# An adaLN modulation moved from VectorE to TensorE, and the softmax division to ScalarE, in a two-layer trunk on one core

## The chip, the core and the metric

The kernel runs on one core of one Trainium2 chip. The metric is the device time of one execution in microseconds (us). The core has five engines with queues of their own: TensorE (PE: matmuls, with its weight loads shown apart as PEld), VectorE (DVE), ScalarE (ACT), GpSimd (POOL) and SyncE (SP), which here issues nearly all transfers from main memory.

## What is computed

The input is 256 tokens of 1,024 float32 values. Layer 0 has an S5 state-space mixer, layer 1 an attention mixer (FoX: softmax attention with a forget gate, 16 heads of 64). Each mixer is followed by a mixture-of-experts block (MoE) of 32 experts in 4 groups, of which a token uses 2. Before each of the four there is a norm and a modulation (adaLN) whose shift and scale come from one conditioning vector c; a gate from c multiplies the result. Keys, values and the forget gate have a norm and a modulation of their own.

```python
def adaln(c, w, b, n):
    mod = jax.nn.silu(c) @ w + b
    return jnp.split(mod, n, axis=-1)

def modulate(h, shift, scale):
    return h * (1.0 + scale[:, None, :]) + shift[:, None, :]
...
    h = modulate(rmsnorm(x, kv_g), shift, scale)
    k, v, fz = jnp.split(h @ kv_w, [D_MODEL, 2 * D_MODEL], axis=-1)
...
    logf = jax.nn.log_sigmoid(fz.astype(jnp.float32) + kv_fb.astype(jnp.float32))
    fcum = jnp.cumsum(logf, axis=1).transpose(0, 2, 1)
...
        logits = (jnp.einsum('bhqd,bhkd->bhqk', qb, kb).astype(jnp.float32) * scale
                  + fcum[:, :, s0:s1, None] - fcum[:, :, None, :s1])
        mask = (s0 + jnp.arange(Q_BLOCK))[:, None] >= jnp.arange(s1)[None, :]
        p = jax.nn.softmax(jnp.where(mask, logits, NEG), axis=-1)
        outs.append(jnp.einsum('bhqk,bhkd->bhqd', p.astype(vb.dtype), vb))
    o = jnp.concatenate(outs, axis=2).transpose(0, 2, 1, 3).reshape(bsz, seq, D_MODEL)
    return (o * jax.nn.sigmoid(og)) @ w_o
```

## The kernel before

**Weights and the ring.** All weights are read once, in 280 blocks of 128 partitions x 8 KB (1 MB each), through a ring of slots. `fetch` takes the next slot and issues the transfer on SyncE's queue (L67), which works in order: a transfer whose slot is not free yet holds up all behind it. The ring has 12 slots; `grow` adds slots where other memory has come free, `shrink` takes them back. `block` fetches a block when it is wanted and `prefetch` earlier. For the second MoE, `load(1)` prefetches expert weights (`wa`, `wb`) as far as there are slots.

**The order of the work.** In the attention stage TensorE's instructions keep the order of the program (`manual_schedule`); those of the other engines and the transfers are put in order by a planner that goes by a model of their times. The order of TensorE is written out in calls near the end of `trunk`: both halves of K (`project(hk, n, head_norm(kn))`), both of V, both of Q, four output gates (`out_gate`), four parts of the output projection (`out_proj`). Small work is put between the matmuls of these loops by generators in the list `between`; `tick` moves the first of them on by one `yield`. `step(ada)` moves on the modulations that are made on TensorE.

**Quarters.** The projections run as float32r products of a high and a low part. `quarter` hands out 512 columns of a weight block at a time: ScalarE copies the high part (L1125), VectorE subtracts it from the weights for the low part (L1126). The last four blocks, `wo`, are first multiplied by a gate on GpSimd (L1123). Up to three quarters stand ready.

**Modulations.** `ada_cols_pe` makes a shift or a scale on TensorE: 64 matmuls over four blocks (L169), and a few VectorE operations that bring the result into columns (`as_columns`). `ada_gate_pe` makes a gate (L184, then L194 and L195). The last shift and scale, those of the second MoE (`ada11`, sets 0 and 1), are made on VectorE instead: `silu_row` spreads silu(c) over a tile (L203, L205), and `ada_cols_v` takes for each 1,024 columns one sum of products (L214), 16 in all. `quarter` calls one such sum at every 9th, later every 4th and 3rd turn; each holds its block's slot until its second sum.

**Normed input.** `hn_parts` transposes the normed tokens (L1153), modulates them (L1160, L1162) and writes high and low parts (L1164, L1165). For K and V it calls `forget_logits` on each chunk as well: small matmuls of 16 columns against `smallw` (L1189), ahead of K's projection (L1200). `forget_gates` takes the logits from there to the running sums.

**Softmax.** `weights(hg)` does one group of four heads, in two query tiles: logits (L1310), mask and maximum on VectorE (L1313, L1317), exponentials on ScalarE (L1319), reciprocal (L1321) and division (L1322) on VectorE. `turned_weights` transposes the result (L1336) and copies it out of PSUM, two of three copies on ScalarE (L1342) and one on VectorE (L1340). `turned_heads` turns keys and queries (L1285), with one of four copies on VectorE (L1289).

In the MoE of layer 0 the ring has slots on the left side of the memory and five on its right; in that of layer 1 on the left alone. Tiles of 8 KB stand one behind another, so all slots of one side begin at the same offset within 256 bytes.

Of the kernel before, what the change touches and what calls it, by code (L numbers as in the profile page):

```python
# [10 lines left out]
F32 = mybir.dt.float32  # L11
# [3 lines left out]
AF = mybir.ActivationFunctionType  # L15
# [4 lines left out]
D = 1024  # L20
T = 256
KD = 8
NE = 32
CAP = 32
NQ = NE // 4
EPS = 1e-6
BIG = 1e30
# [11 lines left out]
def trunk(ctx: ExitStack, tc: tile.TileContext, A, out, ring=12, ring2=4, ring3=5, ring4=3, ring5=4, lpb=2, TK=2):  # L39
# [3 lines left out]

    const = ctx.enter_context(tc.tile_pool(name="const", bufs=1))
    small = ctx.enter_context(tc.tile_pool(name="small", bufs=2))
    wpool = ctx.enter_context(tc.tile_pool(name="ring", bufs=ring))
    slots = [wpool] * ring
    turn_ = [0]
# [126 lines left out]
    def ada_gate_pe(name, j, li, gbc, at_once=False):  # L175
# [16 lines left out]
        for n in range(2):  # L192
            pt = mm_tile()
            PE.matmul(pt, pick[:, n:n + 1].to_broadcast([128, 128]), rows, start=True, stop=True)  # L194
            S.activation(gbc[:, 512 * n:512 * n + 512], pt, AF.Copy)  # L195

    def silu_row(pool):

        o = pool.tile([128, D], F32, name="scr")
        for n in range(2):  # L200
            pt = mm_tile()
            for k in range(4):
                PE.matmul(pt[:, 128 * k:128 * k + 128], sc[:, 4 * n + k:4 * n + k + 1].to_broadcast([128, 128]), ident,  # L203
                          start=True, stop=True)
            S.activation(o[:, 512 * n:512 * n + 512], pt, AF.Copy)  # L205
        return o

    def ada_cols_v(name, j, sc_row, dst, bias, lng=None):

        for b in range(4):  # L210
            w = block(name, j, b)
            for c in range(2):
                wc = w[:, 1024 * c:1024 * c + 1024]
                V.tensor_tensor_reduce(wc, wc, sc_row, 1.0, 0.0, op0=OP.mult, op1=OP.add,  # L214
                                       accum_out=dst[:, 2 * b + c:2 * b + c + 1])
                yield
        V.tensor_tensor(dst, dst, cols[:, bias:bias + 8], op=OP.add)
        if lng is not None:
            V.scalar_tensor_tensor(dst, dst, 1.0, cols[:, lng:lng + 8], op0=OP.add, op1=OP.mult)

    def as_shift(bias, sh):
        return lambda ps: as_columns(ps, 8, sh, cols[:, bias:bias + 8])
# [855 lines left out]
    def add_square(i, n, src):  # L1078
# [1 line left out]
        square(ssq2, i, n)  # L1080

    gb11 = gate_tile(small)
    A2 = [1, 1, 1, 1]
    M.experts(mosti, fill, add_square)


# [7 lines left out]
    gb10 = gate_tile(tp)  # L1094
    ada = [ada_cols_pe("ada10", 0, as_shift(C_ADAB + 32, sh10)),
           ada_cols_pe("ada10", 1, as_gain(C_ADAB + 32, C_LNG + 16, g10)), ada_gate_pe("ada10", 2, 2, gb10, True)]
    fill = [ada_gate_pe("ada11", 2, 3, gb11)]
    later.extend(("ada11", (j, b)) for j in range(2) for b in range(4))
    turns = [0]
    VP = [9, 9, 4, 3]  # L1100


    todo = [("wk", n, kh) for n in range(2) for kh in range(2)] + [("wv", n, kh) for n in range(2) for kh in range(2)]
# [25 lines left out]
    def quarter():  # L1129

        while len(ready) < 3 and (todo or rest_blocks or rest):
            split_next()
        turns[0] += 1
        if turns[0] % VP[turns[0] // 20 % 4] == 0:
            step(vwork)
        return ready.pop(0)


# [4 lines left out]
            while between and next(between[0], 0) == 0:  # L1143
                between.pop(0)

    def hn_parts(xs, sh, g, also=None):

        o = tp.tile([128, KD, 2, T], F32R, tag="hn", name="hn", bufs=1)
        pts = [mm_tile() for _ in range(4)]
        for i in range(2):  # L1150
            for k in range(KD):
                at = 256 * (k % 2) + 128 * i
                PE.transpose(pts[k // 2][:, at:at + 128], xs[:, i, 128 * k:128 * k + 128], ident)  # L1153
        for kk in range(4):
            xf = tp.tile([128, 2, T], F32, tag="xf", name="xf", bufs=2)
            for k2 in range(2):
                k = 2 * kk + k2
                src = pts[kk][:, 256 * k2:256 * k2 + 256]
                if k2:
                    V.tensor_scalar(xf[:, k2], src, g[:, k:k + 1], sh[:, k:k + 1], op0=OP.mult, op1=OP.add)  # L1160
                else:
                    S.activation(xf[:, k2], src, AF.Identity, bias=sh[:, k:k + 1], scale=g[:, k:k + 1])  # L1162
            hi, lo = o[:, 2 * kk:2 * kk + 2, 0, :], o[:, 2 * kk:2 * kk + 2, 1, :]
            S.activation(hi, xf, AF.Copy)  # L1164
            V.tensor_tensor(lo, xf, hi.bitcast(F32), op=OP.subtract)  # L1165
            if also:
                also(kk, xf)
        return o

    in_order = ExitStack()  # L1170
# [1 line left out]
    xs = tp.tile([128, 2, D], F32, tag="xs", name="xs", bufs=1)  # L1172
    for i in range(2):
        rms(ssq2, xs, i)
    scr = silu_row(tp)
    vwork = [ada_cols_v("ada11", 0, scr, sh11, C_ADAB + 48),
             ada_cols_v("ada11", 1, scr, g11, C_ADAB + 56, C_LNG + 24)]
    kn = ap.tile([128, 2, 16, 66], F32, name="kn")
    qn = ap.tile([128, 2, 16, 66], F32, name="qn")
    v = vp.tile([128, 2, D], F32, name="v")  # L1180
    G.memset(kn[:, :, :, 65:66], 1.0)
    G.memset(qn[:, :, :, 64:65], 1.0)
    pz = acc_tile()

    def forget_logits(kk, x):
        for k2 in range(2):
            k = 2 * kk + k2
            for i in range(2):
                PE.matmul(pz[:, 16 * i:16 * i + 16], x[:, k2, 128 * i:128 * i + 128], smallw[:, k, 0:16],  # L1189
                          start=k + i == 0, stop=k == KD - 1, skip_group_check=True)  # L1190

    hk = hn_parts(xs, shkv, gkv, forget_logits)

    def project(src, n, use):
        pk = [acc_tile() for _ in range(2)]
# [40 lines left out]

    def forget_gates():

        def a32(n):
            return ap.tile(t32, F32, name="f_" + n)  # L1240

        fz, fa, fe, fs, f2, fp = (a32(n) for n in ("z", "a", "e", "s", "2", "p"))
        V.tensor_tensor(fz, pz[:, 0:32], cols[:, C_FBR:C_FBR + 32], op=OP.add)
        V.tensor_scalar(fa, fz, -1.0, None, op0=OP.mult)
        V.tensor_tensor(fa, fa, fz, op=OP.min)
        yield
# [29 lines left out]
    def turned_heads(hg):  # L1276

        ts = hts[hg] = []
        for src, nm in ((kn, "kA"), (qn, "qA")):

            dst = ap.tile([66, 4, T], F32, tag=nm, name=nm, bufs=1)
            for i in range(2):
                pt = mm_tile()
                for j in range(4):
                    PE.transpose(pt[:66, 128 * j:128 * j + 128], src[:, i, 4 * hg + j, :], ident)  # L1285
                o = dst[:, :, 128 * i:128 * i + 128]
                s = pt[:66, :].rearrange("p (a t) -> p a t", a=4)
                if nm == "kA" and i:
                    V.tensor_copy(o, s)  # L1289
                elif nm == "kA":  # L1290
                    S.activation(o, s, AF.Copy)
                else:
                    S.activation(o, s, AF.Copy, scale=gqk[:66])
                yield
            ts.append(dst)
    def weights(hg):
# [3 lines left out]
        for qt in range(2):  # L1300
# [18 lines left out]
                S.activation(pr[:, j], pr[:, j], AF.Exp, bias=mx[:, j:j + 1], accum_out=sm[:, j:j + 1])  # L1319
            yield  # L1320
            V.reciprocal(sm, sm)  # L1321
            V.tensor_tensor(pr, pr, sm[:, :, None].to_broadcast([128, 4, w]), op=OP.mult)  # L1322
        yield

    def turned_weights(hg):

        prs = hps.pop(hg)
        if hg > 1:
            while hg - 2 not in done:
                yield  # L1330
        pT = vp.tile([128, 4, 3, 128], F32, tag="pT", name="pT", bufs=2)
        for qt in range(2):
            for kb in range(qt + 1):
                pp = mm_tile()
                for j in range(4):
                    PE.transpose(pp[:, 128 * j:128 * j + 128], prs[qt][:, j, 128 * kb:128 * kb + 128], ident)  # L1336
                dst = pT[:, :, qt + kb, :]
                src = pp.rearrange("p (a t) -> p a t", a=4)
                if kb:
                    V.tensor_copy(dst, src)  # L1340
                else:
                    S.activation(dst, src, AF.Copy)  # L1342
                if qt + kb < 2:
                    yield
        pTs[hg] = pT
# [86 lines left out]
    project(hk, 1, head_norm(kn))  # L1432
    step(ada)
    project(hk, 0, use_v)
    step(ada)
    project(hk, 1, use_v)
    tick(99)
    hq = hn_parts(xs, sh10, g10)
    sgT = tp.tile([128, 8, T], F32, tag="xs", name="sgT", bufs=1)
    project(hq, 0, head_norm(qn))  # L1440
    between += [turned_heads(0), weights(0)]
    step(ada, A2[0])
    project(hq, 1, head_norm(qn))
    for hg in range(1, 4):
        between += [both(turned_heads(hg), turned_weights(hg - 1)), weights(hg)]
    between += [release(), turned_weights(3)]
    step(ada, A2[1])
    out_gate(0)
    step(ada, A2[2])
    out_gate(1)  # L1450
    step(ada, A2[3])
    values(0)
    out_gate(2)
    values(1)
# [3 lines left out]
    split_values(0)  # L1458
    split_values(1)
    out_proj(0)  # L1460
    step(ada, 99)
    values(2)
    split_values(2)
    out_proj(1)
# [4 lines left out]
    grow(er, "ring5", ring5, first=True)  # L1469
    ahead_of_moe()  # L1470
    out_proj(2)
    step(vwork, 99)
    c36 = router(1, sh11, g11)
    out_proj(3)
    in_order.close()
# [25 lines left out]
def layouts(x, c, ln_g, ada_w, ada_b, s5_w_in, s5_lambda_re, s5_lambda_im, s5_log_dt, s5_b_re, s5_b_im,  # L1501
# [69 lines left out]
        return w.reshape(8, 128, n, 256).transpose(2, 1, 0, 3).reshape(n, 128, 2048)  # L1571

    d = {"x": np.asarray(x)[0], "cols": cols, "smallw": smallw, "s5b": s5b, "s5c": s5c}
    def over(w):

        return w.T.reshape(4, 2, 128, D).transpose(0, 2, 1, 3).reshape(4, 128, 2 * D)

    def sets(w, turned=()):
        return np.stack([over(w[:, D * j:D * j + D]) if j in turned else rows(w[:, D * j:D * j + D], 2)
                         for j in range(w.shape[1] // D)])  # L1580

    d["gbias"] = ab[:, 2 * D:].reshape(4, 2, 512)
    d["ada00s"], d["ada00g"] = rows(aw[0][:, :2 * D], 1), sets(aw[0][:, 2 * D:])
    d["ada01"], d["ada10"], d["ada11"] = sets(aw[1]), sets(aw[2]), sets(aw[3], (0, 1))
    d["kvada"] = sets(np.asarray(kv_ada_w))
    d["win"] = bands(np.asarray(s5_w_in[0]))
    w = np.asarray(s5_w_out[0])
# [26 lines left out]
```

## Time and profile before

| | |
|---|---|
| Median of 3 runs | 838.55 us (837.41 to 838.63) |
| The profiled execution: its time | 838.87 us |
| Its span, first to last instruction | 837.1 us |
| Busy TensorE, VectorE, ScalarE, GpSimd | 710.3, 412.0, 218.8, 51.8 us |
| Granted TensorE clock, mean | 0.932 |
| Read from main memory | 297.31 MB |

The span is what the profile's rows cover; 1.8 us of the profiled execution's time lie around it. Busy times of different engines overlap. Instructions of one engine overlap a little too, so that the mean duration of one times their number can exceed the busy time; four matmuls on different column groups run side by side.

### The profile page before, as it was taken

The numbers are of one execution on the slowest core, as the hardware profiler recorded it, in microseconds if no ns is written. First come the engines' busy times: TensorE is split into PE (matmuls) and PEld (weight loads), VectorE is DVE, ScalarE is ACT, GpSimd is POOL, SyncE is SP. The second block draws the span as 40 slices with busy tenths as digits, with TensorE's granted clock in tenths as the row PEclk, the third lists the DMA queues.
The fourth block names the chain that finished last, engine by engine and source line by source line (L and its number), as shares of the span: only waits on it lengthen the run. The fifth ranks groups of instructions, "written<-read, shape, count | busy, mean of one in ns | idle before, by whom it ended". The sixth has DMA issues, their size and how long they took to land. (4 is left out here: it accounts for less than half of the span.)

```text
span 837.1 us, 13449 instructions
## 1 busy us (share of the span) xinstructions
PE 710.3 (85%) x5396; PEld 407.1 (49%) x5396; DVE 412.0 (49%) x1068; ACT 218.8 (26%) x498; POOL 51.8 (6%) x52
## 2 busy tenths in 40 slices
PE   3897999897899987676799988599998999887776
PEld 0674776584343333131286776488764333331311
DVE  7685999864422221120376589967654222221202
ACT  4332333252211110010234355456522111100100
POOL 2000000000000000000002106900000000000000
PEclk9998999998999999898769999789999999997887
DMA  9998956778999999999999996323879999999996
GB/s 370 418 417 346 385 175 254 302 300 324 418 419 420 419 418 420 420 417 416 421 418 377 412 380 230 128 104 105 350 313 404 418 420 419 419 420 419 417 413 251
DMA packets 41827, 299.28 MB, mean 358 GB/s; under 512 B 4632, under 2 KB 4760, under 8 KB 5664
## 3 DMA queue, kind: packets, MB, share of 16 engines
q1 hardware_dynamic: 41344, 297.14, 87.5%
q10 hardware_dynamic: 416, 1.23, 0.4%
q8 instruction: 44, 0.72, 0.3%
q14 instruction: 23, 0.19, 0.1%
HBM read 297.31 MB, written 1.05 MB: 356 GB/s over the span
## 5 line engine op out<-in xcount | busy, mean ns | idle before, releaser
L506 PE MATMUL mm<-w,xg 128*32 128x512 f32 x1024 | 144.3, 645 | 28.7 <-DMA w<-wa 10.9
L506 PEld LDWEIGHTS mm<-w,xg 128*32 128x32 f32 x1024 | 29.8, 112 | 118.2 <-issue 68.1
L478 ACT ACTIVATE xg<-mm,sh,g 128x128 f32<-128x128 f32 x64 | 29.3, 458 | 189.0 <-PE mm L470 172.8
L521 PE MATMUL mm<-w,aT 128*32 128x512 f32 x512 | 68.0, 647 | 12.5 <-DMA w<-wb 6.9
L1200 PE MATMUL acc<-ws,hn 128*128 128x512 f32 x288 | 74.2, 416 | 2.3 <-ACT hn L1164 2.3
L1126 DVE TENSOR_TENSOR ws<-w,ws 128x512 fp32r<-128x512 f32 x80 | 60.9, 765 | 29.6 <-ACT ws L1125 29.3
L470 PE MATMUL mm<-Pr,h 128*128 128x128 f32 x512 | 64.2, 279 | 11.2 <-DVE Pr L458 11.2
L470 PEld LDWEIGHTS mm<-Pr,h 128*128 128x128 f32 x512 | 59.8, 192 | 26.0 <-issue 18.6
L528 PE MATMUL acc<-y,Sc 128*128 128x512 f32 x128 | 65.8, 638 | 6.5 <-DVE y L524 6.5
L1125 ACT ACTIVATE ws<-w 128x512 fp32r<-128x512 f32 x80 | 50.1, 629 | 71.3 <-PE acc L1200 45.9
L1200 PEld LDWEIGHTS acc<-ws,hn 128*128 128x128 f32 x288 | 56.4, 199 | 18.1 <-ACT hn L1164 2.5
L476 DVE TENSOR_SCALAR xg<-mm,g,sh 128x128 f32<-128x128 f32 x64 | 26.2, 410 | 73.1 <-ACT xg L478 73.1
L524 DVE TENSOR_TENSOR y<-mm,gbc 128x512 f32<-128x512 f32 x32 | 22.1, 692 | 68.9 <-PE mm L521 68.6
L489 DVE COPY Sc<-mm 128x256 f32<-128x256 f32 x16 | 6.8, 425 | 86.6 <-PE mm L487 86.6
L511 ACT ACTIVATE a<-mm 128x256 f32<-128x256 f32 x16 | 6.1, 384 | 161.9 <-PE mm L506 161.9
L528 PEld LDWEIGHTS acc<-y,Sc 128*128 128x128 f32 x128 | 22.7, 198 | 47.0 <-issue 29.8
L512 DVE TENSOR_TENSOR a<-a,mm 128x256 f32<-128x256 f32 x16 | 6.7, 420 | 77.5 <-ACT a L511 77.5
L521 PEld LDWEIGHTS mm<-w,aT 128*32 128x32 f32 x512 | 14.1, 113 | 53.0 <-issue 37.1
L981 PE MATMUL acc<-w,uT 128*128 128x512 f32 x64 | 31.9, 645 | 5.7 <-ACT uT L970 5.7
L805 PE MATMUL mm<-hnT,w 128*64 128x128 f32 x512 | 32.4, 286 | 2.7 <-ACT hnT L275 2.7
L805 PEld LDWEIGHTS mm<-hnT,w 128*64 128x64 f32 x512 | 30.7, 140 | 4.4 <-ACT hnT L275 3.7
L1387 PE MATMUL acc<-hn,ws 128*128 128x256 f32 x192 | 28.5, 303 | 2.6 <-DVE ws L1126 2.6
(334 smaller groups left out, 980.9 us busy)
## 6 DMA issues: line engine op xcount, KB each, us to landing
w<-wa SPq DMA_DIRECT2D x128, 1024.0 KB, 19.9
w<-wb SPq DMA_DIRECT2D x64, 1024.0 KB, 19.9
w<-ada SPq DMA_DIRECT2D x36, 1024.0 KB, 10.6
w<-ada00s SPq DMA_DIRECT2D x8, 1024.0 KB, 18.0
w<-kvada SPq DMA_DIRECT2D x8, 1024.0 KB, 9.8
w<-win SPq DMA_DIRECT2D x4, 1024.0 KB
w<-ada00g SPq DMA_DIRECT2D x4, 1024.0 KB, 19.0
w<-woutv SPq DMA_DIRECT2D x4, 1024.0 KB, 17.6
```

The source lines that it names most:

```text
L470: PE.matmul(px[:, 128 * c4:128 * c4 + 128], h[:, i, 128 * c:128 * c + 128], Pr[:, i].rearrange("p a b -> p (a b)"), start=i == 0, stop=i == 1)
L476: V.tensor_scalar(xg[:, c], src, g[:, c:c + 1], sh[:, c:c + 1], op0=OP.mult, op1=OP.add)
L478: S.activation(xg[:, c], src, AF.Identity, bias=sh[:, c:c + 1], scale=g[:, c:c + 1])
L506: PE.matmul(ph[32 * s:32 * s + 32, :], xg[:, k, 32 * s:32 * s + 32], w[:, 512 * s:512 * s + 512], start=k == 0, stop=k == KD - 1)
L521: PE.matmul(py[32 * s:32 * s + 32, :], aT[:, 128 * f + 32 * s:128 * f + 32 * s + 32], w[:, 512 * s:512 * s + 512], start=f == 0, stop=f == 1)
L528: PE.matmul(acc[i][n], scs[q][:, 128 * i:128 * i + 128], y[:, 512 * n:512 * n + 512], start=q == 0, stop=q == NQ - 1, skip_group_check=True)
L805: PE.matmul(ps[64 * v:64 * v + 64, 128 * hh:128 * hh + 128], w[:, k, c0:c0 + 64], hnT[:, k, v::2], start=k == 0 and hh == 0, stop=k == KD ...
L981: PE.matmul(val[t][n], uT[:, m, 128 * t:128 * t + 128], wval[m // 2][:, c0:c0 + 512], start=m == 0, stop=m == 7)
L1125: S.activation(o[:, 0], w, AF.Copy)
L1126: V.tensor_tensor(o[:, 1], w, o[:, 0].bitcast(F32), op=OP.subtract)
L1200: PE.matmul(pk[i], src[:, k, a, 128 * i:128 * i + 128], w[:, b], start=k + a + b == 0, stop=k == KD - 1 and b == 1)
L1387: PE.matmul(po[:, 256 * m2:256 * m2 + 256], w[:, bb, kk, 128 * m2:128 * m2 + 128], hq[:, k, a, :], start=k + a + bb + m2 == 0, stop=k == K ...
```

## The change

- `ada11`'s shift and scale are made by `ada_cols_pe`, after the first and the second output gate; `silu_row`, `ada_cols_v` and the calls in `quarter` go. The weights' layout follows.
- The forget logits leave `hn_parts`. `forget_gates` makes them during the second half of K, from the high and low parts: 16 matmuls with 32 columns of `smallw` as weights, four side by side, a copy on ScalarE, two transposes, and a sum of the four on VectorE.
- The first part of `ada10`'s gate moves from behind the first half of V to behind Q's `hn_parts`.
- The softmax division is done on ScalarE, four instructions for each query tile; the copies of L1289 and L1340 go to ScalarE.
- Two unused tiles ahead of the ring move the left slots by 56 x 4 = 224 bytes and the right ones by 8 x 4 = 32.

```diff
+PAD_LEFT, PAD_RIGHT = 56, 8
...
+    for i, (sd, n) in enumerate((("left", PAD_LEFT), ("right", PAD_RIGHT))):
+        ctx.enter_context(tc.tile_pool(name=f"pad{i}", bufs=1, side=sd)).tile([128, n], F32, name=f"pad{i}")
...
+    ada2 = [ada_cols_pe("ada11", 0, as_shift(C_ADAB + 48, sh11)),
+            ada_cols_pe("ada11", 1, as_gain(C_ADAB + 48, C_LNG + 24, g11))]
...
-        turns[0] += 1
-        if turns[0] % VP[turns[0] // 20 % 4] == 0:
-            step(vwork)
...
-            if also:
-                also(kk, xf)
...
-    scr = silu_row(tp)
-    vwork = [ada_cols_v("ada11", 0, scr, sh11, C_ADAB + 48),
-             ada_cols_v("ada11", 1, scr, g11, C_ADAB + 56, C_LNG + 24)]
...
-    hk = hn_parts(xs, shkv, gkv, forget_logits)
+    hk = hn_parts(xs, shkv, gkv)
...
+        pz = mm_tile()
+        for kh in range(2):
+            for a in range(2):
+                for q in range(4):
+                    k = 4 * kh + q
+                    PE.matmul(pz[32 * q:32 * q + 32, :T], smallw[:, k, 0:32], hk[:, k, a, :].bitcast(F32),
+                              start=kh + a == 0, stop=kh + a == 2)
+        z4 = tp.tile([128, T], F32, tag="xf", name="z4", bufs=2)
+        S.activation(z4, pz[:, :T], AF.Copy)
+        yield
+        pt = mm_tile()
+        for i in range(2):
+            PE.transpose(pt[:, 128 * i:128 * i + 128], z4[:, 128 * i:128 * i + 128], ident)
...
-        V.tensor_tensor(fz, pz[:, 0:32], cols[:, C_FBR:C_FBR + 32], op=OP.add)
+        V.tensor_reduce(fz.rearrange("p (i e) -> p i e", i=2),
+                        pt[:, :T].rearrange("p (i q e) -> p i e q", i=2, q=4)[:, :, 0:16, :], axis=AX, op=OP.add)
+        V.tensor_tensor(fz, fz, cols[:, C_FBR:C_FBR + 32], op=OP.add)
...
-                if nm == "kA" and i:
-                    V.tensor_copy(o, s)
-                elif nm == "kA":
+                if nm == "kA":
                     S.activation(o, s, AF.Copy)
...
-            V.tensor_tensor(pr, pr, sm[:, :, None].to_broadcast([128, 4, w]), op=OP.mult)
+            for j in range(4):
+                S.activation(pr[:, j], pr[:, j], AF.Copy, scale=sm[:, j:j + 1])
...
-                if kb:
-                    V.tensor_copy(dst, src)
-                else:
-                    S.activation(dst, src, AF.Copy)
+                S.activation(dst, src, AF.Copy)
...
     project(hk, 0, use_v)
-    step(ada)
     project(hk, 1, use_v)
     tick(99)
     hq = hn_parts(xs, sh10, g10)
+    step(ada)
...
     project(hq, 0, head_norm(qn))
     between += [turned_heads(0), weights(0)]
-    step(ada, A2[0])
+    step(ada)
...
-    step(ada, A2[1])
     out_gate(0)
-    step(ada, A2[2])
+    step(ada2)
     out_gate(1)
-    step(ada, A2[3])
+    step(ada2)
     values(0)
```

## Rows read from the trace of the kernel before

**Rows 1.** The page: busy time by engine; bandwidth in 40 slices of 20.9 us.

```profile
PE 710.3 (85%) x5396; PEld 407.1 (49%) x5396; DVE 412.0 (49%) x1068; ACT 218.8 (26%) x498; POOL 51.8 (6%) x52
...
GB/s 370 418 417 346 385 175 254 302 300 324 418 419 420 419 418 420 420 417 416 421 418 377 412 380 230 128 104 105 350 313 404 418 420 419 419 420 419 417 413 251
```

**Rows 2.** Stretches in both MoE stages: PE, PEld, DVE, ACT, POOL busy; clock, DMA share, GB/s.

```profile
300.00:350.00 50.00, 38.47 (x257) 14.44 (x255) 8.67 (x22) 4.43 (x10) 0.00 (x0) 0.93 1.01 419
...
700.00:750.00 50.00, 43.61 (x316) 19.67 (x312) 12.34 (x34) 6.26 (x14) 0.00 (x0) 1.00 1.01 419
```

**Rows 3.** SyncE's queue in order of time: start, length, issues.

```profile
543.57 45.81 SPq L67 DMA_DIRECT2D w<-wa  x7
```

**Rows 4.** Stretches of the attention stage, columns as in rows 2.

```profile
487.30:505.70 18.40, 16.09 (x70) 12.43 (x68) 15.32 (x28) 11.68 (x21) 0.00 (x0) 0.91 0.91 355
...
518.90:533.70 14.80, 12.24 (x83) 11.59 (x80) 14.80 (x34) 5.48 (x10) 13.31 (x9) 0.88 0.50 182
533.70:546.00 12.30, 0.04 (x2) 0.04 (x1) 12.30 (x16) 5.35 (x19) 10.96 (x7) 0.59 0.30 113
546.00:560.00 14.00, 14.00 (x102) 13.12 (x103) 8.77 (x30) 6.50 (x17) 0.00 (x0) 0.87 0.31 125
560.00:577.00 17.00, 17.00 (x144) 16.32 (x144) 11.30 (x33) 11.51 (x33) 0.00 (x0) 1.00 0.34 116
577.00:592.00 15.00, 14.31 (x94) 12.15 (x92) 11.90 (x34) 11.32 (x32) 0.00 (x0) 1.00 0.38 133
```

**Rows 5.** TensorE's waits from 414 to 640 us: total, times, longest.

```profile
PE mm L1336 <- issue: 12.3, 1, 12.3
PE acc L1387 <- DVE ws L1126: 2.6, 1, 2.6
PE acc L1200 <- ACT hn L1164: 2.3, 1, 2.3
```

**Rows 6.** TensorE in order of time: start, length, what, idle time before.

```profile
421.11 6.85 PE L1189 MATMUL acc<-smallw,xf 128*128 128x16 f32 x32
...
441.79 3.66 PE L169 MATMUL mm<-w,sc 128*32 128x256 f32 x64
...
472.42 3.64 PE L184 MATMUL mm<-w,sc 128*32 128x512 f32 x32
475.99 11.47 PE L1200 MATMUL acc<-ws,hn 128*128 128x512 f32 x48
487.29 1.91 PE L1153 MATMUL mm<-ident,xs 128*128 128x128 f32 x16
491.51 13.01 PE L1200 MATMUL acc<-ws,hn 128*128 128x512 f32 x48 [2.31 <-ACT hn L1164]
...
628.67 7.07 PE L506 MATMUL mm<-w,xg 128*32 128x512 f32 x64
```

**Rows 7.** The same stretches, L214 alone: length, VectorE busy, clock, DMA share, GB/s.

```profile
505.70:518.90 13.20, 5.17 (x7) 1.00 0.60 204
518.90:546.00 27.10, 8.44 (x10) 0.75 0.41 151
```

**Rows 8.** VectorE by line, 500 to 546 us: busy, mean ns, idle before.

```profile
L1126 DVE TENSOR_TENSOR ws<-w,ws 128x512 fp32r<-128x512 f32 x18 | 18.3, 1027 | 2.2 <-ACT ws L1125 2.1
```

**Rows 9.** GpSimd by line, 430 to 640 us.

```profile
L1123 POOL TENSOR_TENSOR w<-w,gbc 128x512 f32<-128x512 f32 x16 | 27.3, 1741 | 0.0
```

**Rows 10.** VectorE by line, 546 to 605 us.

```profile
L1322 DVE TENSOR_TENSOR pr<-pr,sm 128x1024 f32<-128x1024 f32 x4 | 4.9, 1222 | 0.1
...
L1322 DVE TENSOR_TENSOR pr<-pr,sm 128x512 f32<-128x512 f32 x3 | 2.1, 691 | 0.1
```

**Rows 11.** ScalarE by line, 546 to 605 us.

```profile
L1319 ACT ACTIVATE pr<-pr,mx 128x256 f32<-128x256 f32 x12 | 5.9, 496 | 1.8 <-DVE mx L1317 1.8
L1342 ACT ACTIVATE pT<-mm 128x512 f32<-128x512 f32 x8 | 4.7, 586 | 8.1 <-PE mm L1336 8.1
L1319 ACT ACTIVATE pr<-pr,mx 128x128 f32<-128x128 f32 x12 | 4.7, 390 | 2.9 <-DVE mx L1317 2.9
```

More of the change, by code (lines that the diff above doesn't have):

```diff
@@ L195, in ada_gate_pe @@
             S.activation(gbc[:, 512 * n:512 * n + 512], pt, AF.Copy)
[L197 to L219, printed above, removed]
     def as_shift(bias, sh):
@@ L1082, in trunk @@
     gb11 = gate_tile(small)
-    A2 = [1, 1, 1, 1]
     M.experts(mosti, fill, add_square)
@@ L1096, in trunk @@
            ada_cols_pe("ada10", 1, as_gain(C_ADAB + 32, C_LNG + 16, g10)), ada_gate_pe("ada10", 2, 2, gb10, True)]
+    ada2 = [ada_cols_pe("ada11", 0, as_shift(C_ADAB + 48, sh11)),
+            ada_cols_pe("ada11", 1, as_gain(C_ADAB + 48, C_LNG + 24, g11))]
     fill = [ada_gate_pe("ada11", 2, 3, gb11)]
     later.extend(("ada11", (j, b)) for j in range(2) for b in range(4))
-    turns = [0]
-    VP = [9, 9, 4, 3]
     todo = [("wk", n, kh) for n in range(2) for kh in range(2)] + [("wv", n, kh) for n in range(2) for kh in range(2)]
@@ L1144, in tick, with hn_parts @@
                 between.pop(0)
-    def hn_parts(xs, sh, g, also=None):
+    def hn_parts(xs, sh, g):
         o = tp.tile([128, KD, 2, T], F32R, tag="hn", name="hn", bufs=1)
@@ L1182, in trunk @@
     G.memset(qn[:, :, :, 64:65], 1.0)
[L1183 to L1190, printed above, removed]
-    hk = hn_parts(xs, shkv, gkv, forget_logits)
+    hk = hn_parts(xs, shkv, gkv)
     def project(src, n, use):
@@ L1460, in trunk @@
     out_proj(0)
-    step(ada, 99)
     values(2)
@@ L1471, in trunk @@
     out_proj(2)
-    step(vwork, 99)
+    step(ada2, 99)
     c36 = router(1, sh11, g11)
@@ L1573, in layouts, with sets @@
     d = {"x": np.asarray(x)[0], "cols": cols, "smallw": smallw, "s5b": s5b, "s5c": s5c}
[L1574 to L1580, printed above, removed]
+    def sets(w):
+        return np.stack([rows(w[:, D * j:D * j + D], 2) for j in range(w.shape[1] // D)])
     d["gbias"] = ab[:, 2 * D:].reshape(4, 2, 512)
     d["ada00s"], d["ada00g"] = rows(aw[0][:, :2 * D], 1), sets(aw[0][:, 2 * D:])
-    d["ada01"], d["ada10"], d["ada11"] = sets(aw[1]), sets(aw[2]), sets(aw[3], (0, 1))
+    d["ada01"], d["ada10"], d["ada11"] = sets(aw[1]), sets(aw[2]), sets(aw[3])
     d["kvada"] = sets(np.asarray(kv_ada_w))
```

## Prediction

> **What bounds the kernel now.** Start with the engine line and the slices [rows 1]. No engine is full: TensorE is busy 85% of the span, VectorE 49%. But the slices of bandwidth stand at 416 to 421 GB/s for most of the span, and fall far below it in two places only, the S5 stage early on and the attention stage, at slices 24 to 28 (500 to 605 us). In both mixture-of-experts (MoE) stages the DMA share is 1.01 while TensorE is busy 38 to 44 of 50 us [rows 2]: there the weights set the time, 2.5 us for a block of 1 MB at 418 GB/s. The bytes are the same before and after, so a gain has to come out of time in which the DMA engines stand still, and in the part that the diff touches that is the attention stage.
>
> Why they stand still there is read from SyncE's queue [rows 3]. Seven blocks of the second MoE take 45.8 us to issue, from 543.6 on, where each needs 2.5 us to move: every load waits for a free ring slot. The slots hold weights that attention has not yet used or weights for the MoE, which begins at 628.7 [rows 6]. Slots come free as TensorE moves through attention, so what shortens TensorE's way from 414 to 628.7 moves the slots, the rest of the loads and the end by as much.
>
> So the stage is read by TensorE's waits [rows 5]. One is large: 12.3 us ahead of the transposes of the softmax weights (L1336). The table of stretches [rows 4] shows what is late: from 518.9 to 546 VectorE is busy 27.1 us of 27.1, ScalarE 10.8, while TensorE does nothing from 533.7 to 546. VectorE has a backlog, and the softmax of the first head group stands in it. Of these 27.1 us the adaLN sums that the change removes (L214) hold 8.4, and 5.2 of the 13.2 us before [rows 7]. The rest is made longer by GpSimd: its 16 scalings of the output weights, of 1.7 each [rows 9], run then, and the split of a quarter (L1126) takes 1,027 ns in the mean [rows 8].
>
> **The change, part by part**, in us on TensorE's way; bounds in brackets.
>
> 1. *Forget logits out of the way of K.* Before, 32 small matmuls (L1189) begin at 421.1, as the transposes end, and last 6.9, because each chunk waits for its x; K's first matmul starts behind them. The same step for Q has no logits: its transposes end at 487.29 + 1.91 = 489.2 and the projection starts at 491.5, 2.3 later [rows 6]. K would start at 421.2 + 2.3 = 423.5 where it now starts at about 427.9, up to 4.4 earlier. Chunks that arrive one by one give part of it back (Q's first 48 matmuls take 13.0, the 48 at 476 take 11.5): I take -3.5 (-4.4 to -2.8).
> 2. *The logits again, behind half of K.* 16 matmuls of 256 columns, four side by side. The nearest row has 64 in 3.66 [rows 6], so 0.9, plus two transposes: +1.2 (0.9 to 3.0, if the transposes have to wait for the copy z4). One addition and five small operations on VectorE are covered by the V projections.
> 3. *The gate's matmuls moved from behind V's first half to behind Q's transposes.* They cost 3.64 at either place [rows 6], but now lie in the 2.3 us wait for hn [rows 5]. The granted clock is 0.91 in that stretch [rows 4], 1.6 us of 18.4; I count half of that as won back: -3.1 (-3.8 to -2.3). Their four slots come free some 12 us later, and the queue behind them waits for that long. It costs nothing as long as the loads so put off (the last of wog, ada11, wo) are wanted later still, and they belong to the output gates and the output projection.
> 4. *L214 off VectorE* (16 sums of 1.5 us). The 2.6 us wait for a split at the first output gate goes [rows 5]: -2.6 (-2.6 to 0). Of the 12.3 us wait: VectorE's 27.1 become 27.1 - 8.4 - 0.7 (one division [rows 10]) = 18.0, and that division takes 4 x 0.39 = 1.6 on ScalarE [rows 11]: the weights are ready 19.6 after the same start. TensorE arrives 14.8 - 2.6 + 3.7 (the first of the two new adaLN sets) = 15.9 after it. That leaves 3.7 if VectorE starts as late as now, none if it no longer carries the 5.2 us from before; I take 1.5: -10.8 (-12.3 to -6).
> 5. *The two adaLN sets on TensorE*: 64 matmuls each, the form of L169, 3.66 each [rows 6]: +7.3 (7.3 to 8.5). The first lies in part where the wait was, and that is in step 4's arrival; the second, behind the second output gate, is on the way in full. Their eight slots are held until then, but come free four at a time, and at the place where seven MoE loads waited in [rows 3] as many slots have been given back as before. The row of silu(c) (16 matmuls, two copies) goes too; K's transposes wait for the norm all the same, so I count nothing (0 to -2).
> 6. *Division and copies on ScalarE.* For each later head group 4 x 0.39 + 4 x 0.50 = 3.5 of division, and two copies of 0.6 [rows 11]. ScalarE is busy 29.3 us of the 46 from 546 to 592 [rows 4]; with 3 x (3.5 + 1.2) = 14.1 it stands at 43.4 of 49.7 (the second adaLN set included). That is no bound yet, but a queue in which the splits and the softmax delay each other, where TensorE now has no slack to speak of (busy 14.3 of 15 us at the least). Below: nothing, as VectorE is freed of more than that. Above: each of three groups waits for its 2.7 us more. I take +3 (0 to 8).
> 7. *Aligned slots.* By the sizes of the tiles ahead of them the left slots begin 32 bytes past a multiple of 256 and the right ones 224; they move by 224 and 32 bytes, to 0 and 192. No row shows a transfer into a slot that starts elsewhere, so nothing is counted here; the bound is in the rivals.
>
> [...]
>
> **The sum.** -3.5 + 1.2 - 3.1 - 2.6 - 10.8 + 7.3 + 3.0 = -8.5. The profiled execution took 838.87 us (span 837.1), 0.3 above the median of 838.55: 838.87 - 8.5 = 830.4, so **830**.
>
> **The rivals.**
> - *ScalarE becomes the bound in attention* (step 6 at its upper end, 8 instead of 3, and 3 instead of 1.5 left in step 4): -8.5 + 5 + 1.5 = -2, about 837. For it: 43 of 50 us on an engine that runs in order. Against it: TensorE's busy share there is higher still.
> - *Slower: the large wait stays, because it belongs to GpSimd's scalings and not to L214.* They run where two-input operations of VectorE stretch, and with wo loaded later they run later, beside the second head group. Then step 4's gains go to zero while the matmuls of step 5 are added: -3.5 + 1.2 - 3.1 + 7.3 + 3 = +4.9, about 844. It decides from the point where more than 10 of the 14.9 us of waits in [rows 5] (L1336 and L1387) remain: the sum takes 13.4 of them away and ends at -8.5. Against it: L214 alone is 13.6 us of the stretch.
> - *Aligned slots quicken every load.* About 400 us of the span run at the DMA's pace. The saturated slices differ among themselves by 1% [rows 1], so up to 4 us on top of the sum: 826. Against it: the two MoE stages, one with slots on both sides and one with left slots alone, run alike at 419 GB/s [rows 2].
> - *Hidden anyway*: the loads can't follow the earlier slots, and the end stays. Against it: from 543.6 to 589 only seven were issued.
>
> [...]
>
> **The numbers.** The forecast (826 to 834) has 50%; the aligned slots on top of it (820 to 826) 20%; ScalarE as the bound 15%, of which 10 end below and 5 within 0.2% of 838.6; slower 12%; hidden anyway 3%, all within. A measurement of this kernel tells 0.2% (1.7 us) from no change. That makes faster 0.80, same 0.08, slower 0.12. The range runs from 820, the lower end of the second case, to 838, the upper end of the third; the slower case and a few in 100 below 820 are left out. The bounds of the steps added up give 822 to 847, and the far end needs all of them at once.
>
> **What would show it.** Right: the wait before L1336 under 4 us; VectorE below 90% between the first output gate and those transposes; K's projection 2.3 us behind its transposes; the gate's matmuls (L184) without a wait behind Q's transposes; the second MoE's first matmul at about 620; the rest of the span from there unchanged in length, about 208 us. Step 6 shows as new waits of L1336 or of the output gates for ScalarE, and its busy share above 90% there. Slot alignment shows as slices above 422 GB/s. The prediction is wrong if the wait at L1336 stays above 8 us, if waits for ScalarE add up to over 8, or if the MoE starts earlier while the end stays.

## The result, and the profile after

The changed kernel takes 819.34 us in the median of four runs (819.21 to 819.66), the one before 838.59 beside it: a ratio of 0.9769 [0.975, 0.9788], or 19.4 us less (17.8 to 21.0). That is 10.7 us under the predicted 830 and just under the low end of the range, 820. The profiled execution took 819.66 us with a span of 817.9. One of ten executions of a kernel below, e2, took 1,748.7 us; it is in that kernel's median and not in its ratio.

**The page**, busy time by engine and the slices of bandwidth, which answer to [rows 1]:

```profile
PE 706.3 (86%) x5510; PEld 402.8 (49%) x5510; DVE 381.3 (47%) x1025; ACT 232.1 (28%) x537; POOL 46.7 (6%) x52
...
GB/s 368 426 425 347 406 150 250 292 314 277 426 426 426 426 425 425 428 423 427 424 424 426 315 197 312 204 370 98 349 347 415 426 428 424 427 427 427 425 426 260
```

VectorE has lost 31 us, ScalarE gained 13. What was not forecast is in the other line: the full slices stood at 416 to 421 GB/s and now stand at 423 to 428. The stretches in the two MoE stages, which answer to [rows 2] (columns as there), say the same:

```profile
300.00:370.00 70.00, 56.76 (x370) 22.34 (x362) 13.41 (x36) 6.64 (x15) 0.00 (x0) 0.88 1.01 425
...
700.00:750.00 50.00, 41.98 (x290) 16.34 (x288) 10.99 (x30) 4.42 (x10) 0.00 (x0) 0.97 1.01 427
```

The DMA share is 1.01 as before: the DMA engines are as full as they were and move more.

**TensorE's waits from 400 to 630 us**, which answer to [rows 5]: total, times, longest.

```profile
PE mm L1242 <- DVE f_z L1239: 3.9, 1, 3.9
...
PE acc L1162 <- ACT hn L1140: 0.6, 1, 0.6
PE mm L1314 <- ACT pr L1300: 0.3, 1, 0.3
...
PE acc L1399 <- DVE oT L1391: 0.2, 1, 0.2
```

The wait of 12.3 us ahead of the softmax transposes is gone (the line is L1336 before and L1314 after), and so is the one of 2.6 at the first output gate. One of 3.9 is new: the sums of the forget gates (L1242) wait for VectorE.

**TensorE in order of time**, which answers to [rows 6]:

```profile
415.08 3.97 PE L1129 MATMUL mm<-ident,xs 128*128 128x128 f32 x16 [3.35 <-ACT mm L226]
419.66 13.61 PE L1162 MATMUL acc<-ws,hn 128*128 128x512 f32 x48 [0.62 <-ACT hn L1140]
433.20 3.66 PE L173 MATMUL mm<-w,sc 128*32 128x256 f32 x64
...
443.98 1.93 PE L1207 MATMUL mm<-hn,smallw 128*32 128x256 f32 x32
...
460.99 0.37 PE L1242 MATMUL mm<-f_z,tri 128*128 128x16 f32 x2 [3.89 <-DVE f_z L1239]
...
482.88 1.91 PE L1129 MATMUL mm<-ident,xs 128*128 128x128 f32 x16
485.68 3.64 PE L188 MATMUL mm<-w,sc 128*32 128x512 f32 x32 [0.90 <-DVE xf L1136]
489.25 11.45 PE L1162 MATMUL acc<-ws,hn 128*128 128x512 f32 x48
...
529.10 0.60 PE L1314 MATMUL mm<-ident,pr 128*128 128x128 f32 x4
...
604.31 3.64 PE L188 MATMUL acc<-w,sc 128*32 128x512 f32 x32
...
614.12 7.07 PE L486 MATMUL mm<-w,xg 128*32 128x512 f32 x64
```

From the first MoE's last matmul (its end: 414.27 before, 411.73 now) to the second's first, the attention stage took 214.4 us and takes 202.4. Layer 0 ends 2.5 earlier, and from 614.12 to the end of the span it is 203.8 instead of 208.4. So 12.0 us came out of the stage that the forecast dealt with, where it had 8.5, and 7.2 out of the two stages beside it, where it had nothing.

**Stretches of the attention stage**, which answer to [rows 4]:

```profile
515.10:523.50 8.40, 8.40 (x67) 8.11 (x64) 7.46 (x29) 6.69 (x18) 3.54 (x3) 1.00 0.36 125
523.50:529.10 5.60, 5.60 (x83) 3.94 (x81) 3.94 (x4) 5.60 (x18) 5.35 (x4) 1.00 0.66 208
...
560.00:580.00 20.00, 19.27 (x120) 15.57 (x119) 10.61 (x33) 18.34 (x52) 0.00 (x0) 1.00 0.45 173
```

Between the first output gate and the softmax transposes TensorE works all the time at the full granted clock, where 12.3 us were idle and the clock was 0.59; VectorE is busy 11.4 us of 14.0. On SyncE's queue, against [rows 3], nine blocks are issued in 41.1 us where seven took 45.8:

```profile
541.54 41.09 SPq L71 DMA_DIRECT2D w<-wa  x9
```

### The profile page after: what moved, and what is told of

Same layout as the page of the kernel before. It is cut to its first block, busy times and chain, and to the rows that moved or that the text cites. A ratio compares the mean times of both kernels' runs of the same rounds, so it can differ in the third digit from the quotient of the medians.

```text
span 817.9 us, 13668 instructions
## 1 busy us (share of the span) xinstructions
PE 706.3 (86%) x5510; PEld 402.8 (49%) x5510; DVE 381.3 (47%) x1025; ACT 232.1 (28%) x537; POOL 46.7 (6%) x52
## 5 line engine op out<-in xcount | busy, mean ns | idle before, releaser
L486 PE MATMUL mm<-w,xg 128*32 128x512 f32 x1024 | 141.4, 637 | 24.0 <-DMA w<-wa 10.7
L1105 DVE TENSOR_TENSOR ws<-w,ws 128x512 fp32r<-128x512 f32 x80 | 58.2, 733 | 40.4 <-ACT ws L1104 40.1
L450 PE MATMUL mm<-Pr,h 128*128 128x128 f32 x512 | 65.3, 281 | 11.2 <-DVE Pr L438 11.2
L450 PEld LDWEIGHTS mm<-Pr,h 128*128 128x128 f32 x512 | 60.9, 194 | 26.6 <-issue 19.0
L173 PE MATMUL mm<-w,sc 128*32 128x256 f32 x512 | 29.2, 380 | 0.0
## 6 DMA issues: line engine op xcount, KB each, us to landing
w<-ada SPq DMA_DIRECT2D x36, 1024.0 KB, 10.6
```

What stands on the lines that cost most here:

```text
L173: PE.matmul(ps[32 * q:32 * q + 32, 0:256], sc32(2 * b + kk), bands(w[:, 1024 * kk:1024 * kk + 1024])[:, q], start=b + kk == 0, stop=b == 3 ...
L450: PE.matmul(px[:, 128 * c4:128 * c4 + 128], h[:, i, 128 * c:128 * c + 128], Pr[:, i].rearrange("p a b -> p (a b)"), start=i == 0, stop=i == 1)
L486: PE.matmul(ph[32 * s:32 * s + 32, :], xg[:, k, 32 * s:32 * s + 32], w[:, 512 * s:512 * s + 512], start=k == 0, stop=k == KD - 1)
L1105: V.tensor_tensor(o[:, 1], w, o[:, 0].bitcast(F32), op=OP.subtract)
```

## The experiments

Two theories stood at the start. The prediction's: the whole gain is made in attention, and the alignment of the slots is worth nothing. The rival's: the alignment quickens every load. Later ones are about the backlog of VectorE (L214 or GpSimd's scalings), the forget logits, the gate and the division.

One reading goes through all of them. Kernels with the same code up to the end of the first MoE reach it at different times from profile to profile, 407.5 to 411.7 us with aligned slots. The attention stage is therefore counted from there, and without the 32 matmuls of the gate in the router at its end, which take 3.64 us at the full granted clock, as in the profile after, and up to 6.04 in other runs (last section).

The starts in the second column are worked out from the sizes of the tiles ahead, as in step 7 of the prediction; the profile doesn't show addresses.

| kernel | left slots start at, mod 256 | attention without that gate | layer 0 + rest of the span | median | ratio |
|---|---|---|---|---|---|
| before | 32 | 209.1 | 622.7 | 838.59 | 1 |
| after | 0 | 198.8 | 615.5 | 819.34 | 0.9769 |
| e1, before with aligned slots | 0 | 208.2 | 614.8 | 829.47 | 0.9894 [0.9859, 0.9928] |
| e3, after without | 32 | 199.9 | 619.0 | 826.94 | 0.9869 [0.9836, 0.9902] |
| e2, before | 64 | 208.6 | 620.3 | 838.14 | 1.0004 [0.9986, 1.0022] |
| e10, before | 128 | 208.6 | 620.6 | 837.13 | 0.9986 [0.9967, 1.0004] |
| e9, before | 192 | 206.6 | 622.9 | 837.58 | 0.9994 [0.9978, 1.0009] |
| e11, before | 0 | 208.5 | 615.2 | 830.51 | 0.9893 [0.9862, 0.9923] |
| e13, before | 0 | 209.1 | 615.0 | 829.51 | 0.9882 [0.9851, 0.9913] |
| e4, before without the scalings | 32 | 197.6 | 619.8 | 822.89 (one run) | |
| e5, before with adaLN on TensorE | 32 | 198.1 | 622.2 | 829.17 | 0.9893 [0.986, 0.9926] |
| e6, after, division back | 0 | 199.6 | 611.9 | 818.78 | 0.9759 [0.9737, 0.9781] |
| e8, after, logits back | 0 | 196.9 | 613.6 | 818.20 | 0.9767 [0.9727, 0.9807] |
| e14, after, gate back | 0 | 199.3 | 614.8 | 820.57 | 0.9785 [0.9756, 0.9815] |
| e7, after, sums later | 0 | 193.2 | 611.3 | 813.48 | 0.9713 [0.9687, 0.974] |
| e12, e7 with division back | 0 | 192.9 | 614.2 | 814.53 | 0.9712 [0.9683, 0.974] |

The two columns in the middle are from one profile each; seven kernels with the code of before in this stage scatter by 2.5 us in the first.

### Where the slots begin

Alone on the kernel before (e1), and taken out of the changed one (e3):

```diff
+PAD_LEFT, PAD_RIGHT = 56, 8
...
+    for i, (sd, n) in enumerate((("left", PAD_LEFT), ("right", PAD_RIGHT))):
+        ctx.enter_context(tc.tile_pool(name=f"pad{i}", bufs=1, side=sd)).tile([128, n], F32, name=f"pad{i}")
```

> The kernel before with the two pads alone; nothing else differs. Theory A (the slots' start sets the pace of a load): saturated slices rise from 418 to about 426 GB/s as in the changed kernel, both MoE stages shorten by some 7 us together, ratio about 0.991 to 0.992. Rival (the pace came from other parts of the change, such as other engines' use of the memory): 418 GB/s, ratio 0.998 to 1.002.

> The changed kernel without the pads. Theory A: 418 GB/s again, 7 us slower than the changed kernel, so about 826.5 us, ratio to the kernel before 0.984 to 0.987. Rival (pace from elsewhere): as the changed kernel, 0.977.

The padding alone makes 8.9 us (6.0 to 11.8) of the kernel before, and without it the change keeps 11.0 (8.2 to 13.8); together 19.9, and both at once were measured at 19.4. In e1 the full slices stand at 424 to 428 GB/s and the large wait is still there:

```profile
PE mm L1340 <- issue: 10.7, 1, 10.7
```

So the first theory falls as to the slots, and stands as to attention. Then one constant was changed at a time, PAD_LEFT to 8 (e2), 40 (e9), 24 (e10) and 120 (e13), with PAD_RIGHT as it was, and in e11 PAD_LEFT stayed 56 while the right pad was left out. Theory B, in the expectations of these runs, is that a multiple of 256 counts.

```diff
-PAD_LEFT, PAD_RIGHT = 56, 8
+PAD_LEFT, PAD_RIGHT = 120, 8
```

> As the kernel before, with a left pad of 8 floats instead of 56: left slots begin at 64 past a multiple of 256 (right ones at 192 as in the changed kernel). If a multiple of 64 bytes is what counts: 426 GB/s and the same ratio as with 56 and 8, about 0.992. If a multiple of 256 counts: left slots stay slow, 418 to 420 GB/s in the second MoE, ratio above 0.997.

> The kernel before with a left pad of 40 floats and a right one of 8: all slots begin 192 bytes past a multiple of 256. [...] Rival (some other starts do as well, as the right slots at 192 in the changed kernel seem to): 425 GB/s, ratio near 0.99.

> The kernel before with a left pad of 24 floats and a right one of 8: left slots begin 128 bytes past a multiple of 256. Theory B: 418 to 421 GB/s and the time of the kernel before. Rival (a multiple of 128 is enough): 425 GB/s, ratio near 0.99.

> The kernel before with the left pad of 56 floats alone: left slots at a multiple of 256, the five right ones of the first MoE at 224. Theory B, with a cost of each row by itself: the second MoE at 425 GB/s, the first a little lower, about 424, ratio 0.989 to 0.993. Rival (a few bad rows hold up the others too): the first MoE at 418 to 420, ratio about 0.995.

> The kernel before with a left pad of 120 floats and a right one of 8: left slots begin at an odd multiple of 256 bytes (256 past a multiple of 1,024). Theory B (a multiple of 256 counts): 425 GB/s in both MoE stages, ratio 0.987 to 0.992. Rival (512 or 1,024 counts, which the pad of 56 also gave): 418 to 421 GB/s, ratio 0.998 to 1.002.

The stretch from 700 to 750 us of e2, e10, e9 and e1, then of e13 (the last column is GB/s):

```profile
700.00:750.00 50.00, 42.80 (x312) 18.56 (x308) 12.62 (x34) 6.26 (x14) 0.00 (x0) 1.00 1.01 421
...
700.00:750.00 50.00, 42.66 (x308) 18.30 (x300) 12.62 (x34) 6.26 (x14) 0.00 (x0) 1.00 1.01 421
...
700.00:750.00 50.00, 42.49 (x306) 18.03 (x304) 12.61 (x34) 6.25 (x14) 0.00 (x0) 1.00 1.01 421
...
700.00:750.00 50.00, 40.99 (x288) 16.20 (x284) 11.49 (x32) 4.88 (x11) 0.00 (x0) 0.97 1.01 426
```

```profile
700.00:750.00 50.00, 41.95 (x304) 17.37 (x296) 12.21 (x34) 5.80 (x13) 0.00 (x0) 1.00 1.01 427
```

Starts 64, 128 and 192 bytes past a multiple of 256 give 421 GB/s there and no time; a start at a multiple of 256, an odd one in e13, gives 426 or 427 and 9 to 10 us. No run lies in between. The pads move all tiles of their side that lie behind them, not the slots alone, and no run separates the two; but the gain is in the rate of the loads while the DMA share is 1.01, and the slots are what these loads write. e11 has right slots at 224, as before, and shows in the first MoE the 425 of the changed kernel, whose right slots are at 192:

```profile
300.00:370.00 70.00, 57.16 (x370) 22.59 (x369) 13.07 (x36) 6.64 (x15) 0.00 (x0) 0.88 1.01 425
```

The right pad does nothing that shows. Right slots at a multiple of 256 were not run, so it is open whether slots on the right have a price of their own; e11 and e13 have 425 in this stretch and 427 in the second MoE, but e1, with the starts of the changed kernel, has 426 in both.

### What made VectorE's backlog

e5 makes the two adaLN sets on TensorE in the kernel before, so that `silu_row` goes too, and changes nothing else. e4 leaves out GpSimd's multiplication of `wo` by the gate, so that the output lacks the gate, and keeps L214.

```diff
-    vwork = [ada_cols_v("ada11", 0, scr, sh11, C_ADAB + 48),
-             ada_cols_v("ada11", 1, scr, g11, C_ADAB + 56, C_LNG + 24)]
+    ada2 = [ada_cols_pe("ada11", 0, as_shift(C_ADAB + 48, sh11)),
+            ada_cols_pe("ada11", 1, as_gain(C_ADAB + 48, C_LNG + 24, g11))]
```

> The kernel before with the last shift and scale on TensorE and nothing else (no pads, division and copies on VectorE, logits and gate where they were). Theory A (L214 was enough of the backlog): the waits of L1336 and L1387, 14.9 us, fall to under 3, 7.3 us of matmuls come in, ratio 0.989 to 0.993 (about 831). Rival (the wait belongs to GpSimd's scalings): the wait of L1336 stays above 8 us and the ratio is 1.002 to 1.008.

```diff
-        if name == "wo":
-            G.tensor_tensor(w, w, gate, op=OP.mult)
```

> The kernel before without GpSimd's scaling of wo (L1123 is left out, so the output projection lacks the gate). It tells what the 12.3 us wait of L1336 was made of. If L214's work alone is the backlog, the wait stays above 8 us. If the sharing with GpSimd makes up half of it, L214 takes 1.2 us and L1126 0.69 us each in that stretch, and the wait falls to 2 to 6 us.

In e5 the first softmax transposes don't wait, and two later ones wait 0.6 and 0.7 us. e4's wait there, with all of L214 left:

```profile
PE mm L1334 <- ACT pr L1317: 4.3, 1, 4.3
```

And VectorE by line from 500 to 546 us, of e4 and then of e5 (busy, mean ns), against 1,027 in [rows 8]:

```profile
L1124 DVE TENSOR_TENSOR ws<-w,ws 128x512 fp32r<-128x512 f32 x19 | 12.9, 685 | 3.1 <-ACT ws L1123 3.0
```

```profile
L1126 DVE TENSOR_TENSOR ws<-w,ws 128x512 fp32r<-128x512 f32 x19 | 17.0, 895 | 4.1 <-ACT ws L1125 3.9
```

The split takes 685 ns without GpSimd's multiplications, 895 with them and 1,027 with them and L214. The sums of L214 were stretched in the same way (the kernel before, then e4, same view):

```profile
L214 DVE CUSTOM_DVE_ANT_0 w<-w,scr 128x1024 f32<-128x1024 f32 x8 | 13.7, 1750 | 0.0
```

```profile
L214 DVE CUSTOM_DVE_ANT_0 w<-w,scr 128x1024 f32<-128x1024 f32 x8 | 9.4, 1218 | 0.0
```

Neither theory has it alone: the scalings make these two operations of VectorE longer by a third to a half, and L214 is work that then no longer fits. To take either away empties most of the backlog. In the attention stage e5 makes -11.0 us by the table, the whole change -10.3; in time e5 makes 9.0 (6.2 to 11.7) and the change without pads 11.0 (8.2 to 13.8). So the move of the sums to TensorE is, as far as these numbers tell, all of the gain there, and a gain of the other parts together isn't shown.

### Forget logits, gate, division

e8 puts the logits back into `hn_parts`, on the changed kernel:

```diff
-    hk = hn_parts(xs, shkv, gkv)
+    hk = hn_parts(xs, shkv, gkv, forget_logits)
```

> The changed kernel with the forget logits made in hn_parts again, ahead of K. By the traces the move gave 6.0 us at K's start and cost 7.8 behind it: 1 to 3 us faster than the changed kernel, 816.5 to 818.5, ratio 0.974 to 0.976. By the predicted sizes (-3.5 and +1.2) it would be 2.3 slower, 821.6, ratio 0.980.

It takes 818.20, a ratio of 0.9767 against the 0.9769 of the changed kernel. Its interval of 6.7 us holds both expectations, so the time decides nothing, and the 1.9 us less in attention by the table lie within the scatter there. The order of time shows why neither place wins by much: K starts later, and V meets no wait for the sums.

```profile
417.01 6.85 PE L1162 MATMUL acc<-smallw,xf 128*128 128x16 f32 x32
423.70 13.65 PE L1173 MATMUL acc<-ws,hn 128*128 128x512 f32 x48
...
457.36 0.29 PE L1236 MATMUL mm<-f_z,tri 128*128 128x16 f32 x2
```

e7 keeps the logits where the change has them and lets TensorE come to the sums one step of the list later, so that V's matmuls run while VectorE works:

```diff
         yield
+        fzs.append(fz)
+    fzs = []
+    def forget_sums():
+        fz = fzs[0]
         pc = mm_tile()
...
     project(hk, 1, head_norm(kn))
+    between.append(forget_sums())
```

> The changed kernel with the matmuls of the running sums of the forget gate behind the key norm of K's second half, five quarters later. Theory A (the 3.9 us wait of L1242 for f_z, and the lower clock behind it, lie on TensorE's way): the wait goes, 814 to 816, ratio 0.971 to 0.974. Rival (the slots' order holds the loads there, so that TensorE's gain is lost): as the changed kernel, 0.977.

```profile
411.20 1.06 PE L1129 MATMUL mm<-ident,xs 128*128 128x128 f32 x8 [3.35 <-DMA w<-wk]
...
458.66 0.37 PE L1249 MATMUL mm<-f_z,tri 128*128 128x16 f32 x2 [0.46 <-DVE f_z L1239]
...
459.10 0.38 PE L1251 MATMUL mm<-f_z,tri 128*128 128x16 f32 x2
459.32 14.24 PE L1162 MATMUL acc<-ws,hn 128*128 128x512 f32 x60
473.40 1.91 PE L1129 MATMUL mm<-ident,xs 128*128 128x128 f32 x16
```

The wait is 0.5 us instead of 3.9, the way from K's transposes to Q's 62.2 us instead of 67.8 (473.40 - 411.20, 482.88 - 415.08), and the time 813.48. That is about 5 us under the changed kernel (4.7 by the ratios, 5.9 by the medians), with intervals that don't overlap, and e7 is faster than the kernel before and the changed one. e7 shows the point: the move keeps its gain at K only if nothing waits for what was moved.

e14 puts the gate's first part back behind V's first half:

```diff
     project(hk, 0, use_v)
+    step(ada)
     project(hk, 1, use_v)
...
-    step(ada)
```

> The changed kernel with the gate's first part behind the first half of V again. By the trace the move gave 3.0 us: 821 to 823.5, ratio 0.979 to 0.982, with a wait of about 2 us for hn at Q's start. Rival (the 3.9 us wait at the running sums, which comes before it, or the slots' order, swallows the difference): within 1.5 us of the changed kernel, 0.977.

1.2 us slower in the median, 0.5 longer in attention, with intervals that overlap: the sign is as expected, the size is small, and the difference isn't clear of noise. The waits for `hn`, Q's and K's together:

```profile
PE acc L1162 <- ACT hn L1140: 2.2, 2, 1.6
```

e6 gives the division and the two copies back to VectorE, e12 the division on top of e7:

```diff
-            for j in range(4):
-                S.activation(pr[:, j], pr[:, j], AF.Copy, scale=sm[:, j:j + 1])
+            V.tensor_tensor(pr, pr, sm[:, :, None].to_broadcast([128, 4, w]), op=OP.mult)
```

> The changed kernel with the softmax division and the two copies on VectorE again. Theory A (with L214 gone VectorE has room): within 2 us of the changed kernel, 818 to 821, ratio 0.976 to 0.979. Rival (moving them to ScalarE was needed): 823 or more, with a wait of L1314 for VectorE.

> The changed kernel with the running sums later (as in the run of that name) and the softmax division on VectorE again; copies stay on ScalarE. If the division's place makes no difference: 812 to 815, ratio 0.969 to 0.973, as with the sums alone. If ScalarE had been a bound (its waits at L1322 and the oT split): 1 to 3 us faster. If VectorE still is one: 816 or more.

Both medians lie within 0.2% of their partners', and the intervals overlap. From 560 to 580 us VectorE and ScalarE are busy 15.4 us of 20 each in e6, against 10.6 and 18.3 in the changed kernel, and TensorE 19.3 in both:

```profile
560.00:580.00 20.00, 19.32 (x125) 16.47 (x124) 15.43 (x41) 15.38 (x41) 0.00 (x0) 1.00 0.54 201
```

## Why the prediction was off, step by step

**Step 7 (aligned slots, counted at nothing) is the step that failed**, by about 8 us (19.4 less with the pads, 11.0 without; 8.9 to 9.9 on the kernel before), and it alone carries the time out of the range: without the pads the change takes 826.94, inside the 826 to 834 forecast for the likeliest case. Nothing was counted because no row showed a slot that starts elsewhere; the argument against the rival was that the two MoE stages, with slots that begin at 32 and 224 bytes in the first and at 32 alone in the second, run alike at 419 GB/s [rows 2]. That compared two starts of which neither is a multiple of 256, and says nothing on one that is. The rival named the right cause and its bound of 4 us was half of the size, since it was taken from the scatter among slices that all had the slow start. From the rates the size comes out: 400 us of full slices, 419 against 426 GB/s, 1.7% or 6.6 us; by the table layer 0 and the rest of the span take 619.0 to 622.9 us in the seven kernels whose slots start elsewhere and 611.3 to 615.5 in the nine with aligned slots. No trace here shows why a start elsewhere is slower; from 700 to 750 us the rate is 419 GB/s at 32 (420 in e3) and 421 at 64, 128 and 192.

**Step 1 (logits out of K's way)** was mis-sized: -3.5 forecast, -6.3 found. K's last transposes in the kernel before:

```profile
419.61 1.70 PE L1153 MATMUL mm<-ident,xs 128*128 128x128 f32 x8 [0.94 <-DVE xs L254]
```

From the end of K's transposes to the end of K's first half it was 441.79 - 421.31 = 20.5 us (the logits of [rows 6] start 0.2 ahead of that end) and is 433.20 - 419.05 = 14.2 (the transposes end at 415.08 + 3.97). K's projection begins 0.6 us behind the transposes, not the 2.3 of Q, which was the row taken for it.

**Step 2 (logits behind half of K)** was mis-sized by more: +1.2 forecast, about +7.8 found. From there to Q's transposes the way is 2.15 us shorter (65.98 to 63.83), and 3.64 of gate has left it, so steps 1 and 2 together cost 1.5. With step 1 at -6.3 this leaves 7.8. The logits take 1.93 of it: the forecast took 16 matmuls as a quarter of a row of 64, but that row stands for 32 calls in the kernel, two rows to a call, and the 16 calls leave the 32 rows of L1207. Two transposes take 0.38 and the wait for the sums 3.89. Most of the rest is the granted clock behind that wait. V in the changed kernel, then in the kernel before, then the changed kernel's clock:

```profile
461.65 21.39 PE L1162 MATMUL acc<-ws,hn 128*128 128x512 f32 x84
```

```profile
462.45 10.04 PE L1200 MATMUL acc<-ws,hn 128*128 128x512 f32 x42
```

```profile
461.00:465.00 4.00, 4.00 (x15) 3.27 (x16) 0.33 (x3) 0.63 (x1) 0.00 (x0) 0.62 1.01 429
```

At the pace of the kernel before, where the clock is 1.00, the 84 would take 20.1 us, 1.3 less; 0.3 stays open. "Covered by the V projections" was the error. TensorE stands still in V's first half until VectorE's chain is through, because the order of TensorE is fixed; e7 shows it by moving that one place, and its clock is 1.00 from 459.3 to 473.3 us.

**Step 3 (gate moved)** had -3.1. Against the kernel before, the part from Q's transposes to the end of Q's first half fits. Against e14, which has all but this move, the same part is 1.0 us shorter with the gate's 3.64 counted, and the time 1.2. With the gate back the wait for Q's `hn` is 1.6, not 2.3, and the granted clock from 470 to 500 us is 1.00 (0.91 in the stretch of [rows 4]): the slack that it was to fill had shrunk. e5 has the same 1.6 and 1.00, so it is the move of the sums that took it. The gate's matmuls don't start at once either: they wait 0.9 us for VectorE (`xf`).

**Steps 4 and 5 (sums from VectorE to TensorE)** were right in mechanism and mis-sized: -13.4 + 7.3 = -6.1 forecast, -11.0 in e5's attention and 9.0 us (6.2 to 11.7) in its time. No wait is left ahead of the first transposes, where 1.5 was taken, the 2.6 at the output gate is gone as well, and TensorE runs at the full granted clock from 515 to 529 us, where in the stretches of [rows 4] it had 0.88 and 0.59, and 0.87 behind them. By those rows the lower clock cost an estimated 3.3 us of TensorE's work (0.12 of 12.24 and 0.13 of 14.00), a term that the sum didn't have; with the 1.5, and 0.7 less of waiting for Q's `hn`, that is about the 4.9 between -6.1 and -11.0. The matmuls cost what [rows 6] gave, 3.66 a set. The rival that the wait belongs to GpSimd was half right (e4), but its condition, that the wait stay when L214 goes, was not met.

**Step 6 (division and copies on ScalarE)** had +3 and is worth nothing that can be told. ScalarE is at 92% from 560 to 580 us, above the 90% named as its sign, but the one wait for it there is 0.3 us (L1314); the other, 0.2 (L1399), is for VectorE. A division costs on ScalarE what its exponentials do, as was taken (ScalarE by line and shape, the changed kernel from 528 to 592 us):

```profile
L1300 ACT ACTIVATE pr<-pr,sm 128x256 f32<-128x256 f32 x15 | 6.4, 499 | 0.2 <-DVE sm L1298 0.2
L1296 ACT ACTIVATE pr<-pr,mx 128x256 f32<-128x256 f32 x12 | 5.9, 497 | 2.5 <-DVE mx L1294 2.5
```

For the wider tile that puts four instructions of 499 ns in the place of one of 1,222 on VectorE [rows 10]; in e6 and e12 the time is the same on either engine, within 0.2% of the medians.

So without the slots the forecast of -8.5 lies inside what e3 measured, 11.0 less (8.2 to 13.8), but in part by luck, since errors of both signs cancel: steps 1, 4 and 5 gave more, step 6 cost less, and steps 2 and 3 took most of that back. Of the signs that were named, the second MoE's first matmul came at 614.1 instead of 620, and the 208 us from there became 203.8, by the slots.

## What to carry to other kernels

Look at the start address of every tile that large transfers write, before any of the fine work: in these stages, where the DMA engines were full, two unused tiles that moved the slots to a multiple of 256 bytes were worth nearly as much as all the rest of the change (8.4 to 11.0 us). To say that a thing makes no difference, the rows compared must include one of each kind; two rows that share the fault look alike. And where an engine has a fixed order, a piece of work that is moved takes its consumer with it: move that too, or the wait comes back in the next loop, as in step 2.

## What the runs showed of the hardware that was not expected

The rate of transfers from main memory into on-chip memory, with rows of 8 KB and all engines full, has two levels here: 419 to 421 GB/s where the left slots start 32, 64, 128 or 192 bytes past a multiple of 256, 425 to 427 where they start at one, even or odd (300 to 370 and 700 to 750 us; 32 in before and e3, 64, 128 and 192 in e2, e10 and e9, a multiple in after, e1, e7, e11 and e13).

TensorE's granted clock in the router differs between kernels with the same code there. The changed kernel from 600 to 616 us, then e6, with e6's gate in order of time after that:

```profile
600.00:616.00 16.00, 13.38 (x120) 8.83 (x123) 8.24 (x49) 3.59 (x11) 1.17 (x2) 1.00 0.80 325
```

```profile
600.00:616.00 16.00, 14.10 (x97) 7.68 (x101) 8.31 (x49) 2.62 (x7) 1.17 (x2) 0.79 0.66 253
```

```profile
602.54 6.04 PE L188 MATMUL acc<-w,sc 128*32 128x512 f32 x32
```

The 32 matmuls take 3.64 us where the stretch is at 1.00 and 6.04 where its mean is 0.79. In the 15 us ahead of them TensorE was busy 14.2 in both kernels, with the same pause of 0.78 us for the router's `hT`. The eight matmuls right behind that pause (L362) take 1.92 us in e6 and 1.08 in the changed kernel, the 32 of L450 behind the gate 4.04 in both; what makes the difference stays open. This one step differs by 2.4 us between the two, as much as several terms of the sum.
